# Quartering a second of the seven gate/up products in a FoX hybrid block on one Trainium2 core

## The chip, the cores and the metric

The kernel runs on one core of a Trainium2 chip. That core has a matrix engine (PE, with its weight loads shown as PEld), three engines for elementwise work (VectorE, called DVE in the profile; ScalarE, called ACT; GpSimd, called POOL), and a queue for transfers that SyncE (SP) issues. Matmuls write into banks of PSUM, an accumulator memory; everything else lies in SBUF, or in DRAM. Each engine works through its own queue in the order of the program, and waits there for the others.

The metric is the device time of one execution in microseconds. The kernel before takes 1034.87 us, the median of three runs (1034.17 to 1035.08).

## The reference

One layer on x of 1024 rows by 1024 channels, in float32:

```python
h = rmsnorm(x, norm1_g)
proj = einsum('bsd,de->bse', h, w_in)        # q, k, v, f_logit, u
attn = forgetting_attention(q, k, v, log_sigmoid(f_logit + b_forget))
pool = multiscale_pool(u, w_pool, pool_scale)
x = x + einsum('bse,ed->bsd', concat(attn, pool), w_out)
h2 = rmsnorm(x, norm2_g)
gate = einsum('bsd,df->bsf', h2, w_gate)     # w_gate, w_up: 1024 x 2816
up = einsum('bsd,df->bsf', h2, w_up)
x = x + einsum('bsf,fd->bsd', silu(gate) * up, w_down)
return rmsnorm(x, final_g)
```

The change concerns `gate`, `up` and `silu(gate) * up`, and the sums of the latter on which the product with `w_down` works.

## The kernel before

**Precision.** A float32 product is made of three matmuls in a reduced format: each operand is split into a high half (a copy in that format, on ACT, L120) and a low half (the operand less its high half, on DVE, L121). `mm3` multiplies high by high, low by high and high by low (L161 to L163).

**The gate/up product.** The 2816 channels are taken in 11 pairs `j` of 2 x 128 channels. For each pair, the weights are a 2 x 2 matrix of blocks `a11`, `a12`, `a21`, `a22` (by pair half and by half of the 1024 inputs; each 128 x 2 x 512, gate and up side by side), and the activations are a 2 x 2 matrix of blocks too (by input half and by half of the rows). One level of Strassen-Winograd makes the pair's output with seven products P1 to P7 instead of eight. P1, P2 and P4 take weight blocks as they are; P5, P6, P7 and P3 take sums `s1` to `s4` of them (L1070 to L1073, on POOL). A product has two parts, gate (n = 0) and up (n = 1), of twelve matmuls of 512 columns each. Its moving side is a block of activations, split once for all pairs (`b11`, `b21`, `t2`, `t3`, `t1`, `b22`, `t4`); its weights are a *page* of high and low halves, made per pair. Three pages rotate.

**Quartering.** From pair 1 on, P3 is again cut into seven fine products Q1 to Q7, by the same scheme, 42 matmuls of 256 columns in all. Their weights are two smaller pages, P3a (four quarters: Q1, Q2, Q7, Q4) and P3b (three: Q5, Q3, Q6), whose sums are made in place in `s4` (L1213). Each fine product is added by DVE from its PSUM bank into a snapshot in SBUF (L1249).

**Banks, snapshots, corners.** P1, P6, P5 accumulate in the bank pair `c1`; after each of them ACT copies the banks into a snapshot (`sn`: `sP1`, `sU2`, `sU4`; L1135). P2 has the banks `c2`, P7 and P4 the banks `c3`. The four corners of a pair's output (`h11`, `h12`, `h21`, `h22`) are the snapshots plus a bank: DVE adds gate and up (L1154, L1156), ACT applies silu to the gate (L1155), POOL multiplies (L1157). The down product needs, by the same scheme, the corners and their sums `f1` to `f4` (L1161, on POOL). All are sent to DRAM (`hsd`) by DMAs that ACT's queue issues (`spill`, L1254).

**The order.** The program lists for each pair `LATER = P1 P2 P6 P7 P5 P3a P4 P3b`, and walks through it. At each step it makes the page of the step after next (`next_page`), issues spills, emits the step's matmuls, and then the corners that have become complete (`after`). P4 and the fine products of P3 are laid among each other by hand. `tc.issue_after` pins an instruction behind another in its queue; otherwise each engine runs the instructions in the order in which the program emits them. Raw weights are loaded per half (`gu_raw`), by SP's queue.

**Around it.** Before the pairs come the input projection, attention, pooling and the output projection; after them come the down product and the last norm. The change touches there only which tiles the row buffers and the first down pages use.

## Time and profile before

| | before |
|---|---|
| median of three runs | 1034.87 us |
| the profiled execution's time | 1035.78 us |
| its span in the profile | 1034.0 us |
| PE busy | 1022.9 us, 99% |
| DVE busy | 711.6 us, 69% |
| ACT busy | 465.2 us, 45% |
| POOL busy | 405.4 us, 39% |
| granted TensorE clock, mean | 0.998 |
| time in DMA queue q1 (weights, corners, rows) | 33.0% of 16 engines |

The span is the time between the first and the last record; the execution's own time is 1.78 us longer. A line of a timeline gives the start and duration in us, the engine, the line in the kernel, the operation with what it writes and reads, and in brackets how long the engine was idle before and what ended that. A line of the windows gives, for PE, PEld, DVE, ACT and POOL, the busy time and (in brackets) how many instructions began, and at its end the granted clock, the share of DMA and GB/s. A line of the waits gives who waited for whom: us in total, how often, and the longest. A duration in a timeline is from an instruction's start to its end; the next one of the same engine can start a little before that.

### The profile page before, as it was taken

The numbers are of one execution on the slowest core, as the hardware profiler recorded it, in microseconds if no ns is written. First come the engines' busy times: TensorE is split into PE (matmuls) and PEld (weight loads), VectorE is DVE, ScalarE is ACT, GpSimd is POOL, SyncE is SP. The second block draws the span as 40 slices with busy tenths as digits, with TensorE's granted clock in tenths as the row PEclk, the third lists the DMA queues.
The fourth block names the chain that finished last, engine by engine and source line by source line (L and its number), as shares of the span: only waits on it lengthen the run. The fifth ranks groups of instructions, "written<-read, shape, count | busy, mean of one in ns | idle before, by whom it ended". The sixth has DMA issues, their size and how long they took to land.

```text
span 1034.0 us, 14701 instructions
## 1 busy us (share of the span) xinstructions
PE 1022.9 (99%) x5284; PEld 873.6 (84%) x5284; DVE 711.6 (69%) x1131; ACT 465.2 (45%) x747; POOL 405.4 (39%) x316
## 2 busy tenths in 40 slices
PE   8999999999999999999999999999999999999997
PEld 7988888998888888888888888888888888888885
DVE  7565566776886479786565455556547899788886
ACT  7434355665665257533343333433334343333346
POOL 4350121213346043356558548557558410000045
PEclk9999999999999999999999999999999999999999
DMA  7214424333743133333242243233326665352424
GB/s 251 53 47 144 105 80 106 82 103 86 234 166 104 49 132 112 93 112 102 102 142 101 65 142 106 79 122 112 92 102 254 214 254 181 119 188 94 153 92 163
DMA packets 108249, 130.25 MB, mean 126 GB/s; under 512 B 7368, under 2 KB 70352, under 8 KB 108176
## 3 DMA queue, kind: packets, MB, share of 16 engines
q1 hardware_dynamic: 96544, 108.18, 33.0%
q10 hardware_dynamic: 11072, 19.69, 5.0%
q0 software_dynamic: 560, 1.44, 0.4%
q8 instruction: 42, 0.69, 0.3%
q14 instruction: 31, 0.25, 0.1%
HBM read 86.29 MB, written 33.03 MB: 115 GB/s over the span
## 4 chain that ended last, share of the span: by engine, by line
PE 49%; DVE 2%; DMA 1%; issue 1%; POOL 1%; ACT 0%; SPq 0%; POOLq 0%; ACTq 0%; DVEq 0%
PE gu_P L163 9%; PE gu_P L162 9%; PE gu_P L161 9%; PE d L162 5%; PE d L163 5%; PE d L161 5%; DMA r_wd<-in_w_down_dram 1%; DVE d L121 1%; DVE x2f_s L1533 0%; DMA r<-in_w_up_dram 0%; POOL f L1161 0%; DMA hsdP<-f 0%; DVE gu_P_l L121 0%; POOL h L1157 0%; POOL hsdP L1254 0%
## 5 line engine op out<-in xcount | busy, mean ns | idle before, releaser
L162 PE MATMUL d<-d,d 128*128 128x512 f32 (+1 forms) x308 | 118.8, 389 | 0.5 <-DVE d L121 0.5
L163 PE MATMUL d<-d,d 128*128 128x512 f32 (+1 forms) x308 | 118.5, 388 | 0.0
L629 POOL TENSOR_SCALAR p<-p,rr 128x128 f32<-128x128 f32 (+3 forms) x64 | 48.5, 763 | 177.0 <-DVE rr L628 135.9
L161 PE MATMUL d<-d,d 128*128 128x512 f32 x308 | 107.8, 388 | 0.0
L120 ACT ACTIVATE d<-r_f 128x1536 fp32r<-128x1536 f32 (+1 forms) x28 | 38.7, 1383 | 109.6 <-PE d L162 106.0
L1157 POOL TENSOR_TENSOR h<-h,qh 128x512 f32<-128x512 f32 x33 | 64.5, 1955 | 34.8 <-ACT qh L1155 26.9
L1070 POOL TENSOR_TENSOR s<-r 128x1024 f32<-128x1024 f32 x10 | 24.0, 2397 | 133.0 <-DMA r<-in_w_up_dram 86.9
L121 DVE TENSOR_TENSOR gu_P_l<-r,gu_P_h 128x1024 fp32r<-128x1024 f32 x32 | 52.8, 1651 | 31.9 <-ACT gu_P_h L120 31.9
L120 ACT ACTIVATE gu_P_h<-r 128x1024 fp32r<-128x1024 f32 x32 | 33.8, 1060 | 85.9 <-issue 43.4
L162 PEld LDWEIGHTS d<-d,d 128*128 128x128 f32 x308 | 57.8, 188 | 13.3 <-DVE d L121 1.4
L1438 POOL TENSOR_SCALAR sse<-sse 128x1 f32<-128x1 f32 x7 | 3.5, 494 | 167.3 <-ACT junk L1434 167.3
L161 PEld LDWEIGHTS d<-d,d 128*128 128x128 f32 x308 | 57.8, 188 | 12.0
L163 PEld LDWEIGHTS d<-d,d 128*128 128x128 f32 x308 | 57.8, 188 | 11.8
L121 DVE TENSOR_TENSOR gu_P_l<-s,gu_P_h 128x1024 fp32r<-128x1024 f32 (+1 forms) x38 | 51.8, 1371 | 18.9 <-ACT gu_P_h L120 18.8
L626 ACT ACTIVATE p<-p,mn 128x128 f32<-128x128 f32 (+3 forms) x64 | 49.4, 772 | 32.3 <-DVE mn L620 29.4
L648 DVE TENSOR_TENSOR tl<-tp,th 128x512 fp32r<-128x512 f32 (+1 forms) x80 | 49.5, 633 | 9.7 <-ACT th L647 8.7
L121 DVE TENSOR_TENSOR d<-r_f,d 128x1536 fp32r<-128x1536 f32 (+1 forms) x28 | 47.7, 1705 | 6.2 <-ACT d L120 6.2
L163 PE MATMUL qk<-hTh,l_qk 128*128 128x512 f32 x128 | 50.7, 396 | 0.0
L161 PE MATMUL qk<-hTh,h_qk 128*128 128x512 f32 x128 | 50.6, 395 | 0.0
L162 PE MATMUL qk<-hTl,h_qk 128*128 128x512 f32 x128 | 50.4, 394 | 0.0
L1155 ACT ACTIVATE qh<-qh 128x512 f32<-128x512 f32 x33 | 20.9, 632 | 64.6 <-POOL f L1161 32.6
L1533 DVE TENSOR_TENSOR x2f_s<-d,x2f_s 128x512 f32<-128x512 f32 x64 | 42.5, 686 | 10.6 <-PE d L163 10.6
(802 smaller groups left out, 3235.8 us busy)
## 6 DMA issues: line engine op xcount, KB each, us to landing
r_f<-hsdP SPq DMA_DIRECT2D x77, 256.0 KB
r_wd<-in_w_down_dram SPq DMA_DIRECT2D x22, 512.0 KB
r<-in_w_gate_dram SPq DMA_DIRECT2D x21, 512.0 KB
r<-in_w_up_dram SPq DMA_DIRECT2D x21, 512.0 KB
hsdP<-f ACTq DMA_DIRECT2D x40, 256.0 KB
s<-hi SPq DMA_DIRECT2D x64, 128.0 KB
hsdP<-h ACTq DMA_DIRECT2D x32, 256.0 KB
x<-in_x_dram SPq DMA_DIRECT2D x8, 512.0 KB
```

The costliest lines, as they stand in the source:

```text
L120: mark["hi"] = nc.scalar.activation(out=hi, in_=src, func=AF.Copy)
L121: return eng.tensor_tensor(out=lo, in0=src, in1=f32(hi), op=ALU.subtract)
L161: nc.tensor.matmul(ps, lh, rh, start=start, stop=False, **kw)
L162: nc.tensor.matmul(ps, lh, rl, start=False, stop=False, **kw)
L163: mark["mm"] = nc.tensor.matmul(ps, ll, rh, start=False, stop=stop, **kw)
L626: nc.scalar.activation(out=pr[:, :n], in_=pr[:, :n], func=AF.Exp, scale=-1.0, bias=mn, accum_out=rs)
L629: nc.gpsimd.tensor_scalar(out=pr[:, :n], in0=pr[:, :n], scalar1=rr, scalar2=1.0, op0=ALU.mult, op1=ALU.mult)
L648: nc.vector.tensor_tensor(out=tl[:, :w], in0=tp[:, :w], in1=f32(th[:, :w]), op=ALU.subtract)
L1070: g(out=s1, in0=a21, in1=a22, op=ALU.add)
L1155: nc.scalar.activation(out=q, in_=q, func=AF.Silu)
L1157: nc.gpsimd.tensor_tensor(out=h, in0=h, in1=q, op=ALU.mult)
L1533: added = nc.vector.tensor_tensor(out=row, in0=ps, in1=row, op=ALU.add)
```

## The change

- **P4 is quartered like P3**, in pairs 2 to 10. Pair 1, whose P3 was quartered before, now has seven whole products. The fine pieces of P4 are laid among the matmuls of P7, those of P3 among P5's (`PIECES`). The order of a pair is now `P2 P1 P6 P4a P7 P4b P3a P5 P3b`.
- **The fine products' banks.** Q1, Q6 and Q5 share a bank (A), Q7 and Q4 one (B), Q2 and Q3 one (C). For P4, A and B come from the rotating pair `m`, and C is P2's first bank; for P3, A is P2's second bank and B and C come from `m`. Q5 is added into two targets instead of one. P4's fine products are added into the snapshot `sU2`; those of P3 into a new pair of tiles `acc`, four of them by a copy on ACT (L1270) and the others by DVE (L1273).
- **The corners are made in place**: the snapshot takes the bank's add (`add_bank`, L1310), the silu (L1318) and POOL's product (L1319), with no tile of its own.
- **The weight sums move from POOL to DVE** and are made in place in the raw blocks, in two pairs: `small_sums` (L1069, L1070) at the pair's start, `large_sums` (L1076, L1077) two steps later. `s` serves P6 and then P3; `a21` becomes P7's operand, `a11` P5's.
- **Raw weights are loaded block by block** as their homes become free.
- The quartered block of P4's moving side (`t4`) is made on DVE as `b22`'s is, in pair 1, and `b22`'s after it.

```diff
-    LATER = ("P1", "P2", "P6", "P7", "P5", "P3a", "P4", "P3b")
-    todo = [(j, k) for j in range(NG) for k in (LATER if j else FIRST)]
+    LATER = ("P2", "P1", "P6", "P4a", "P7", "P4b", "P3a", "P5", "P3b")
+    todo = [(j, k) for j in range(NG) for k in ((FIRST, PRODUCTS)[j] if j < 2 else LATER)]
...
+    PIECES = (
+        ("Q1", "Q2", "Q7", (0, (0, 1)), "Q4"), ((0, (2, 3)), "Q6", (1, (0, 1)), (1, (2, 3))), ("Q3", "Q5"),
+    )
...
-        elif i and (k in ("P3a", "P3b") or k == "P4" and j):
+        elif j > 1 and in_pair > 2:
+            small, whole = (("P4", "P7"), ("P3", "P5"))[in_pair > 5]
...
+            acc = snaps[j, "sU2" if small == "P4" else "acc"]
+            for piece in PIECES[in_pair % 3]:
```
```diff
-    def gu_sums(j):
+    def small_sums(j):
+
         a11, a12, a21, a22 = gu_parts(j)
-        s1, s2, s3, s4 = (xw_tile(f"s{i}", f"s{i}_{j}", (P, 2, 512)) for i in (1, 2, 3, 4))
-        g = nc.gpsimd.tensor_tensor
-        g(out=s1, in0=a21, in1=a22, op=ALU.add)
-        g(out=s2, in0=s1, in1=a11, op=ALU.subtract)
-        g(out=s3, in0=a11, in1=a21, op=ALU.subtract)
-        g(out=s4, in0=a12, in1=s2, op=ALU.subtract)
-        return dict(P1=a11, P2=a12, P6=s2, P7=s3, P5=s1, P3=s4, P4=a22)
+        both = xw_tile("s1", f"s_{j}")
+        operands[j].update(P6=both, P3=both)
+        nc.vector.tensor_tensor(out=a21, in0=a11, in1=a21, op=ALU.subtract)
+        nc.vector.tensor_tensor(out=both, in0=a22, in1=a21, op=ALU.subtract)
+
+    def large_sums(j):
+
+        a11, a12, _, _ = gu_parts(j)
+        both = operands[j]["P6"]
+        nc.vector.tensor_tensor(out=a11, in0=both, in1=a11, op=ALU.add)
+        nc.vector.tensor_tensor(out=both, in0=a12, in1=both, op=ALU.subtract)
```
```diff
-    FINE_BANK = dict(Q1="A", Q6="A", Q5="A", Q3="A", Q7="B", Q4="B", Q2="C")
-    FINE_TO = dict(Q1=(0, 0), Q2=(0, 0), Q7=(1, 1), Q4=(1, 0), Q6=(1, 0), Q5=(1, 1), Q3=(0, 1))
+    FINE_BANK = dict(Q1="A", Q6="A", Q5="A", Q7="B", Q4="B", Q2="C", Q3="C")
+    FINE_TO = dict(
+        Q1=((0, 0),), Q2=((0, 0),), Q7=((1, 1),), Q4=((1, 0),), Q6=((1, 0),), Q3=((0, 1),), Q5=((0, 1), (1, 1))
+    )
+    FINE_COPY = ("Q1", "Q7", "Q4", "Q3")
+    FINE_AT = dict(
+        P4=dict(A=("m", 2), B=("m", 2), C=(BANKS["c2", 0], 1)), P3=dict(A=(BANKS["c2", 1], 1), B=("m", 2), C=("m", 2))
+    )
...
+        for n, h in FINE_TO[q]:
+            out = acc[n][:, QTR[h]]
+            if k == "P3" and q in FINE_COPY:
+                nc.scalar.activation(out=out, in_=ps, func=AF.Copy)
+                continue
+            with tc.issue_after(mark["add"].ins) if "add" in mark else ExitStack():
+                mark["add"] = nc.vector.tensor_tensor(out=out, in0=ps, in1=out, op=ALU.add)
...
+    def gated(j, name, key, ts, src=None):
+
+        for n, t in enumerate(ts):
+            if src:
+                add_bank(t, src, n)
+            if n == 0:
+                nc.scalar.activation(out=t, in_=t, func=AF.Silu)
+        nc.gpsimd.tensor_tensor(out=ts[1], in0=ts[1], in1=ts[0], op=ALU.mult)
+        feats[name] = ts[1]
+        if key:
+            spills.append((hsd[key, j], ts[1]))
```

**Three places in the queues**, all in the middle pairs. A name holds its pair: `gu6_P5_l` is the low half of the page of P5 in pair 6, `fineA_6P4` the bank A of P4's fine products in pair 6; the last digits are a tile's number.

DVE, before, pair 6, from P4's low half through P3's fine adds to the next pair's P1:

```order
L121 TENSOR_TENSOR gu6_P4_l_6871<-r1_6_6575,gu6_P4_h_6870 128x1024
L1154 TENSOR_TENSOR qh22_6_6906<-gu6_P70_6844,sn6_sU40_6901 128x512
L1249 TENSOR_TENSOR sn6_sU40_6901<-fineA_6P3_6927,sn6_sU40_6901 128x256
L121 TENSOR_TENSOR gu6_P3b_l_6915<-s4_6_6622,gu6_P3b_h_6914 128x768
L1156 TENSOR_TENSOR h22_6_6905<-gu6_P71_6857,sn6_sU41_6903 128x512
L1249 TENSOR_TENSOR sn6_sU40_6901<-fineC_6P3_6935,sn6_sU40_6901 128x256
L1249 TENSOR_TENSOR sn6_sU41_6903<-fineB_6P3_6943,sn6_sU41_6903 128x256
L1249 TENSOR_TENSOR sn6_sU41_6903<-fineA_6P3_6927,sn6_sU41_6903 128x256
```

DVE, in the changed kernel, pair 6, from Q3 of P4 (bank C) to the first add of P3's fine products:

```order
L1273 TENSOR_TENSOR sn6_sU20_6993<-fineC_6P4_7015,sn6_sU20_6993 128x256
L121 TENSOR_TENSOR gu6_P5_l_7083<-a11_6_6748,gu6_P5_h_7082 128x1024
L1273 TENSOR_TENSOR sn6_sU20_6993<-fineA_6P4_7007,sn6_sU20_6993 128x256
L1310 TENSOR_TENSOR sn6_sU21_6994<-gu6_P71_7063,sn6_sU21_6994 128x512
L121 TENSOR_TENSOR gu6_P3b_l_7110<-s_6_6880,gu6_P3b_h_7109 128x768
L1273 TENSOR_TENSOR sn6_sU21_6994<-fineA_6P4_7007,sn6_sU21_6994 128x256
L1273 TENSOR_TENSOR acc6_0_7114<-fineC_6P3_7124,acc6_0_7114 128x256
```

Q5's two adds (bank A, rows 3 and 6) now stand with a page's low half ahead of the first, and an add from P7's bank and another low half between them. Q7 of P3 is the next to use bank A of P4.

DVE again, in the changed kernel, from the first low half of pair 7 to its second sum of weights:

```order
L121 TENSOR_TENSOR gu7_P2_l_7154<-a12_7_6958,gu7_P2_h_7153 128x1024
L1310 TENSOR_TENSOR sn6_sP70_7076<-gu6_P10_6922,sn6_sP70_7076 128x512
L1273 TENSOR_TENSOR acc6_1_7115<-fineA_6P3_7116,acc6_1_7115 128x256
L1310 TENSOR_TENSOR sn6_sP71_7077<-gu6_P11_6935,sn6_sP71_7077 128x512
L121 TENSOR_TENSOR gu7_P1_l_7187<-a11_7_7086,gu7_P1_h_7186 128x1024
L1069 TENSOR_TENSOR a21_7_6965<-a11_7_7086,a21_7_6965 128x1024
L1273 TENSOR_TENSOR acc6_0_7114<-fineA_6P3_7116,acc6_0_7114 128x256
L1273 TENSOR_TENSOR acc6_1_7115<-fineA_6P3_7116,acc6_1_7115 128x256
L1070 TENSOR_TENSOR s_7_7218<-a22_7_7004,a21_7_6965 128x1024
```

The same stretch before, from the next pair's P1 on:

```order
L121 TENSOR_TENSOR gu7_P1_l_6978<-r0_7_6841,gu7_P1_h_6977 128x1024
L1249 TENSOR_TENSOR sn6_sU41_6903<-fineA_6P3_6927,sn6_sU41_6903 128x256
L121 TENSOR_TENSOR gu7_P2_l_7001<-r0_7_6841,gu7_P2_h_7000 128x1024
L1213 TENSOR_TENSOR s4_7_6921<-s4_7_6921 128x256
L1249 TENSOR_TENSOR sn6_sU40_6901<-fineA_6P3_6927,sn6_sU40_6901 128x256
L1154 TENSOR_TENSOR qh21_6_7014<-gu6_P70_6844,sn6_sU20_6832 128x512
L1156 TENSOR_TENSOR h21_6_7013<-gu6_P71_6857,sn6_sU21_6834 128x512
L121 TENSOR_TENSOR gu7_P6_l_7028<-s2_7_6919,gu7_P6_h_7027 128x1024
```

The first sum of the pair's weights (L1069) has come in ahead of Q5's last two adds, whose bank is P2's second one.

ACT, before, from P1's second snapshot of pair 6 on to P3a's high half:

```order
L1135 ACTIVATE sn6_sP11_6765<-gu6_P11_6750 128x512
L1254 DMA hsdP2_5_4835<-h21_5_6714 128x512
L1254 DMA hsdP5_5_4868<-f1_5_6720 128x512
L1155 ACTIVATE qh11_6_6798<-qh11_6_6798 128x512
L1254 DMA hsdP6_5_4846<-f2_5_6722 128x512
L120 ACTIVATE gu6_P5_h_6803<-s1_6_6619 128x1024
L1254 DMA hsdP7_5_4857<-f3_5_6724 128x512
L1254 DMA hsdP3_5_4879<-f4_5_6726 128x512
L1135 ACTIVATE sn6_sU20_6832<-gu6_P10_6737 128x512
L1254 DMA hsdP1_6_4825<-h11_6_6797 128x512
L120 ACTIVATE gu6_P3a_h_6837<-s4_6_6622 128x1024
```

ACT, in the changed kernel, the same transfers of pairs 5 and 6:

```order
L1278 DMA hsdP5_5_4874<-f1_5_6872 128x512
L1306 ACTIVATE sn6_sP10_6948<-gu6_P10_6922 128x512
L1278 DMA hsdP6_5_4852<-f2_5_6874 128x512
L120 ACTIVATE gu6_P7_h_6961<-a21_6_6627 128x1024
L1278 DMA hsdP7_5_4863<-f3_5_6876 128x512
L1306 ACTIVATE sn6_sP11_6949<-gu6_P11_6935 128x512
L1318 ACTIVATE sn6_sP10_6948<-sn6_sP10_6948 128x512
L1278 DMA hsdP3_5_4885<-f4_5_6878 128x512
L1306 ACTIVATE sn6_sU20_6993<-gu6_P10_6922 128x512
L1278 DMA hsdP1_6_4831<-sn6_sP11_6949 128x512
L120 ACTIVATE gu6_P4b_h_7000<-a22_6_6666 128x768
L1306 ACTIVATE sn6_sU21_6994<-gu6_P11_6935 128x512
```

The transfer of f3 now stands ahead of P1's second snapshot instead of behind it, and the transfer of h11 (`hsdP1`) ahead of P4b's high half.

More of the change, by code (lines that the diff above doesn't have):

```diff
@@ L1205, in fine_steps, with own_temps, ring_temps @@
         ]
+    def own_temps():
+        pair = const.tile([P, 2, 2, 256], F32, tag="wmask", bufs=1, name="pair")
+        ends = [wk.tile([P, 2, 256], F32, tag=f"e{n}", bufs=1, name=f"end{n}") for n in range(2)]
+        return lambda c, h: (pair[:, h, :, :], ends[h])[c]
+    def ring_temps(c, h):
+        return wk_tile("h", 8, f"whole{c}{h}").rearrange("p (c t) -> p c t", c=2)
     def fine_page(j, k, part):
@@ L1288, in tile_kernel @@
     BANK3 = (("m", 2), ("m", 2), ("tp1", 1), ("po", 1))
-    PAGES = (("t3h", "t3l", "t1h", "t1l"), ("b22h", "b22l", "t4h", "t4l"))
+    PAGES = (("t3h", "t3l", "t4h", "t4l"), ("b22h", "b22l", "t1h", "t1l"))
     SUMS = dict(P5="b21h", P6="b21l", P7="t2h", P4="t2l")
@@ L1395, in tile_kernel @@
                     down_page(0)
[L1396 to L1399 removed]
+        if (j, k) == (1, "P1"):
+            fine_tiles("t4", dict(Q5=((xw, "s2"),), Q6=((xw, "s3"),), Q7=((xw, "s4"),)))
+            finer += fine_steps("t4", own_temps())
+        if (j, k) == (1, "P4"):
+            while finer:
+                finer.pop(0)()
+            fine_tiles("b22", dict(
+                Q5=((const, "wmask"),), Q6=((wk, "e0"), (wk, "e1")), Q7=((wk, "e2"), (xw, "junk2"))
+            ))
+            finer += fine_steps("b22", ring_temps)
+        for _ in range(min(3, len(finer) - (j == 1 and k != "P4"))):
+            with tc.issue_after(mark["page"].ins):
+                finer.pop(0)()
         pages.pop((j, k))
```

190 lines of the change are left out of this document (111 added, 79 removed).

## The prediction

> **What bounds the kernel now.** I read the page's sums first, then the windows by stage, then the timelines of one pair's stretch.
>
> ```profile
> span 1034.0 us, 14701 instructions
> PE 1022.9 (99%) x5284; PEld 873.6 (84%) x5284; DVE 711.6 (69%) x1131; ACT 465.2 (45%) x747; POOL 405.4 (39%) x316
> ...
> 649.73:687.51 37.78, 37.78 (x187) 32.05 (x187) 20.83 (x26) 13.91 (x19) 22.99 (x11) 1.00 0.32 105
> ...
> 800.00:1034.00 234.00, 226.16 (x1023) 187.44 (x1021) 200.44 (x209) 94.96 (x105) 40.60 (x45) 0.99 0.46 161
> ```
>
> PE is busy 1022.9 of 1034.0 us. One pair of the gate and up products lasts 37.78 us, in which PE never waits; DVE is busy 20.83, POOL 22.99, ACT 13.91, at a granted clock of 1.00. So only two things count here: the matmul time of a pair, and any new wait of PE.
>
> ```profile
> 653.42 0.39 PE L161 MATMUL gu_P<-t1h,gu_P_h 128*128 128x512 f32 x1
> ...
> 654.10 0.28 PE L161 MATMUL fineA_6P<-b22h,gu_P3a_h 128*128 128x256 f32 x1
> ...
> 654.69 0.28 PE L163 MATMUL fineA_6P<-b22h,gu_P3a_l 128*128 128x256 f32 x1
> ...
> 656.13 0.28 PE L163 MATMUL fineB_6P<-fine3h_b,gu_P3a_l 128*128 128x256 f32 x1
> 656.25 0.40 PE L161 MATMUL gu_P<-t4h,gu_P_h 128*128 128x512 f32 x1
> ```
>
> From 653.42 to 654.10 three whole matmuls start, 0.2275 us each; from 654.10 to 656.25 eighteen fine ones, 0.1195 each. A whole product is 24 × 0.2275 = 5.46 us, a quartered one 42 × 0.1195 = 5.02. Six and one make 37.78, the window.
>
> **What the quartering gains.** 5.46 - 5.02 = 0.44 us for each product. Pairs 2 to 10 quarter one more, pair 1 one less: 8 × 0.44 = 3.5 us, 0.34% of the time. A pair without waits is 5 × 5.46 + 2 × 5.02 = 37.34 us. That is all there is to win; one wait of 0.44 us in a pair takes it back.
>
> **What DVE gets.**
>
> ```profile
> 655.01 0.42 DVE L1249 TENSOR_TENSOR sn_sU<-fineA_6P,sn_sU 128x256 f32<-128x256 f32 x1 [2.04 <-PE fineA_6P L163]
> 655.36 0.95 DVE L121 TENSOR_TENSOR gu_P3b_l<-s,gu_P3b_h 128x768 fp32r<-128x768 f32 x1
> 656.22 0.69 DVE L1156 TENSOR_TENSOR h<-gu_P,sn_sU 128x512 f32<-128x512 f32 x1
> 656.82 0.42 DVE L1249 TENSOR_TENSOR sn_sU<-fineC_6P,sn_sU 128x256 f32<-128x256 f32 x1
> ...
> 670.92 1.22 DVE L121 TENSOR_TENSOR gu_P_l<-s,gu_P_h 128x1024 fp32r<-128x1024 f32 x1
> 672.05 1.79 DVE L1273 TENSOR_TENSOR sn_sU<-sn_sU,sn_sU 128x512 f32<-128x512 f32 x1
> ...
> 684.99 1.22 DVE L1213 TENSOR_TENSOR s<-s 128x256 f32<-128x256 f32 x3
> ```
>
> From start to start, in a row without gaps: low half of 1024 1.13, of 768 0.86; add from a bank of 512 0.60, of 256 0.34 (0.33 to 0.35); 256 out of SBUF 0.40 (1.22 for three, to the last one's end), taken as 0.34 from start to start. A sum of 1024 on DVE has no row; it has the low half's shape and two SBUF inputs, so I take 1.13 (bounds: 0.86, the low half of 768, and 2.08 us, what a low half of 1024 takes beside POOL, below). Per pair: 7 × 1.13 + 2 × 0.86 + 4 sums × 1.13 + 20 × 0.34 + 8 × 0.60 = 25.8 us of 37.3. DVE fits on average; the order of its queue decides. POOL loses four sums of 2.4 us a pair, which nothing waits for late today, so that is worth nothing by itself.
>
> **Wait 1: P3's Q7, 1.79 us a pair.** Q7 of P3 writes the bank that held Q1, Q6 and Q5 of P4, free after Q5's second add. Put Q3's end at 0. Row 654.69 ends at 654.97, 0.16 us behind the start of the next piece (654.81), and DVE starts at 655.01: so DVE starts at 0.20. In the queue then stand Q3's add 0.34, P5 low 1.13, Q5's first add 0.34, an add from P7's bank 0.60, P3b low 0.86, Q5's second add 0.42 to its end: 3.89. PE has Q5, Q1 and Q2 of 0.72 each, and is due at 2.15. With 0.05 of release it goes on at 3.94: **1.79 lost**. Nothing here hangs on a guess but the order, and DVE's rows run in it. In the kernel before, the fine products that use those banks next come a whole pair later, so there these adds have time.
>
> **The lock between DVE and POOL.**
>
> ```profile
> 661.03 1.30 POOL L1157 TENSOR_TENSOR h<-h,qh 128x512 f32<-128x512 f32 x1
> 662.28 3.39 POOL L1071 TENSOR_TENSOR s<-s,r 128x1024 f32<-128x1024 f32 x1
> 665.75 3.26 POOL L1073 TENSOR_TENSOR s<-r,s 128x1024 f32<-128x1024 f32 x1
> ...
> 677.47 1.29 POOL L1161 TENSOR_TENSOR f<-h,sn_sU 128x512 f32<-128x512 f32 x1
> ...
> 679.96 2.28 POOL L1157 TENSOR_TENSOR h<-h,qh 128x512 f32<-128x512 f32 x1
> ```
> ```profile
> 661.66 1.76 DVE L121 TENSOR_TENSOR gu_P_l<-r,gu_P_h 128x1024 fp32r<-128x1024 f32 x1 [0.60 <-ACT gu_P_h L120]
> ...
> 679.00 2.08 DVE L121 TENSOR_TENSOR gu_P_l<-s,gu_P_h 128x1024 fp32r<-128x1024 f32 x1 [2.15 <-ACT gu_P_h L120]
> ```
> ```profile
> 580.73 2.41 POOL L1070 TENSOR_TENSOR s<-r 128x1024 f32<-128x1024 f32 x1 [11.11 <-DMA r<-in_w_up_dram]
> ...
> 581.26 0.42 DVE L1249 TENSOR_TENSOR sn_sU<-fineC_4P,sn_sU 128x256 f32<-128x256 f32 x1
> ```
>
> A DVE low half that begins during a POOL operation ends some 1.1 us after that one (662.33 to 663.42), and POOL's next, of 3.39 instead of 2.4, ends late in its turn: they take turns by whole instructions. The add with a bank (581.26) beside POOL takes its plain 0.42. So each POOL operation of 1.25 us among DVE's two-SBUF-input operations can cost them up to 1.25 us. The Trainium skill ("SBUF — State Buffer", section "Who interferes with whom") says the same, an exclusive lock of the shared port pair for a whole instruction; by a shared bandwidth, its opposite, the forecast would be rival A's.
>
> **Wait 2: P2's second half, 1.0 us a pair.** Its bank is free after Q5's adds of the P3 before, which stand behind P1 low and the first sum. After wait 1, PE ends P5's last matmul at 11.71 and comes to P2's second half at 15.72 (3.94 + 5 fine products of 0.717 + 36 × 0.2275). DVE adds P5's bank at 11.75 to 12.43; POOL's gate product follows at 12.51, P1 low is ready at 12.6. If POOL comes first: 13.80 + 1.13 + 1.13 + 0.34 + 0.42 = 16.8, a loss of 1.0; if DVE does, 15.7 and none. I take POOL, as the earlier by 0.1 us, and keep both.
>
> **Wait 3, from the lock, 1.15, and wait 4 at P4's Q4, 2.4 us.**
>
> ```profile
> 645.19 0.33 ACTq L1254 DMA_DIRECT2D hsdP<-h  x1
> 645.57 1.06 ACT L120 ACTIVATE gu_P3a_h<-s 128x1024 fp32r<-128x1024 f32 x1 [1.62 <-POOL h L1157]
> ...
> 654.13 0.84 ACT L120 ACTIVATE gu_P3b_h<-s 128x768 fp32r<-128x768 f32 x1 [0.49 <-PE gu_P L162]
> ...
> ACT gu_P3a_h L120 <- POOL h L1157: 14.6, 9, 1.6
> ```
>
> Spills are issued from ACT's queue and wait for POOL; the next high half waits behind them (1.62 us here, nine times 14.6 in all, today hidden by pages made early). From 16.7 on, DVE has in order: a sum 1.13, two bank adds 1.20, 0.34, P6 low and P4a low 2.26, a sum 1.13, 0.34, a sum 1.13, then 0.34 × 3 and a bank add 0.60, P7 low 1.13, P1's second bank add 0.60: 10.9 us, to 27.6. Into it fall POOL's gate product and f1 to f4, five of about 1.1: 33.2. Two things follow. A spill of f3 on ACT stands ahead of the snapshot of P1's second bank, which P6's second half writes on: about 1.15 us. And POOL's product of h11 ends at 34.5, its spill holds ACT to 35.0, P4b high takes 0.75, P4b low 0.86, and Q2's and Q7's adds behind it 0.34 each: 37.4. PE needs Q7's bank, to write Q4, at 35.0: 2.4 lost. Bounds for both together: nothing, if POOL's operations fall into DVE's gaps; 5 × 1.25 more than now if all of them stretch it further.
>
> **The sum.** 37.34 + 1.79 + 1.0 + 1.15 + 2.4 = 43.7, against 37.78: 5.9 more, and for four restarts, whose first matmul takes 0.50 instead of 0.39 (below), some 0.1 in all: 6.0.
>
> ```profile
> 855.05 0.50 PE L162 MATMUL d<-d,d 128*128 128x512 f32 x1 [0.45 <-DVE d L121]
> ```
>
> 9 × 6.0 = 54. Pair 1 loses its quartering, 0.44. The quartering of the two blocks runs on DVE in pairs 1 and 2, some 25 operations of 512 at 0.6 to 1.8 us: 0 to 5 us seen by PE, 3.5 taken, as it lies in the queue ahead of page halves. At the last pair two column sums stand in DVE's queue: 0 to 2, 1 taken. Together 59. The profiled execution took 1035.78 us, 1.78 more than its span and 0.91 more than the median of 1034.87: 1035.78 + 59 - 0.91 = **1094 us**.
>
> **The rivals.** *A: only the waits that DVE's own order makes; the lock is absorbed.* For it: POOL has 10 us of work a pair instead of 23, and may slip between DVE's waits. Against it: the rows show strict turns, and POOL's five lie where DVE has no gap. 9 × (1.35 to 2.35) + 0.44 gives 1047 to 1056; with part of waits 3 and 4, up to 1075. *B, the other side: faster.* The place is P3's Q7: if the chain of six on DVE ended before 2.15 instead of 3.89, as it would with the two low halves (1.99) behind Q5's second add, wait 1 would be gone, and with waits 2 to 4 hidden 3.5 us remain: 1031. Against it: the order stands in the program, and a bank that is read late is not written early. The point of decision is 0.4 us of waits a pair: above it the result is slower. *C: longer.* More than the forecast's turns, or a lower clock: PE idles 14% of a pair. The last window of the first fence had 7.8 us of PE idle at a clock of 0.99, so short waits cost none there. If every pair lost 2 to 4 us more: 1112 to 1130. The Trainium skill ("TensorE: Matmul & The Clock Gate", "What's actually happening") halves the clock after an idle window of about 3.4 us; the longest wait that I forecast is 2.4 us, so by it none would fall into that, unless waits run together. That the quartering isn't done is no rival: the program's order has the fine matmuls.
>
> **How the numbers follow.** Forecast 65% (1075 to 1112, 1094 likeliest), A 18% (1047 to 1075), C 10%, B 5%, within 0.2% (about what a measurement can tell from no change) 2%. 1047 to 1112 leaves out 17%. Slower: 93%.
>
> **What would show it.** A window of one pair of 43 to 44 us with 37.3 of PE busy. In the waits: PE on a DVE add at P3's Q7 for 9 × 1.8 = 16 us; PE at P2 on DVE for 9; PE at P4's Q4 on DVE for 20 to 24; ACT behind POOL at spills. Matmul pitches unchanged. It would be wrong if Q7 starts within 0.5 us of Q2's end, if DVE's sums take other than 1.0 to 2.1 us, or if POOL's rows beside them show no stretch.

## The result, and the profile after

The changed kernel takes **1100.66 us** (median of six runs, 1099.47 to 1103.74), against 1034.97 us (six runs, 1034.17 to 1035.91) for the kernel before: a ratio of 1.064, with an interval of 1.0623 to 1.0658. It is 65.7 us slower. The forecast was 1094 us, with a range of 1047 to 1112.

The page's sums, and then the waits of PE as who waited for whom (us in total, times, longest):

```profile
span 1099.3 us, 15266 instructions
PE 1035.2 (94%) x5428; PEld 879.5 (80%) x5428; DVE 817.3 (74%) x1270; ACT 486.3 (44%) x795; POOL 318.6 (29%) x284
```
```profile
PE gu_P L161 <- ACT sn_sP L1306: 7.7, 9, 2.4
PE gu_P L161 <- DVE acc L1273: 7.2, 8, 0.9
PE fineB_10P L161 <- DVE sn_sU L1273: 5.7, 2, 3.8
...
PE fineB_6P L161 <- DVE sn_sU L1273: 4.0, 2, 2.4
```

Four kinds of wait are new. Each pair has two at bank B (`fineB`), one at P2's second half (for `acc`), and one at P6 (for P1's snapshot on ACT). PE's busy time rose too, by 12.3 us, though it has less matmul work: matmuls at half clock, and the matmuls on both sides of a wait, count for more (0.27 us a wait, below). DVE is busy 105.7 us longer and is at 74%, so it isn't the bound on average.

Now one pair, from P3's Q7 to the next one's. The PE timeline's waits between 645 and 690, where the bracket at a row's end is how long PE was idle before it, and the windows of this pair and the one after it:

```profile
645.35 0.39 PE L161 MATMUL fineB_5P<-fine_b22Q7h,gu_P3a_h 128*128 128x256 f32 x1 [1.62 <-DVE sn_sU L1273]
...
658.37 0.50 PE L161 MATMUL gu_P<-b21h,gu_P_h 128*128 128x512 f32 x1 [0.89 <-DVE acc L1273]
...
670.22 0.50 PE L161 MATMUL gu_P<-t2h,gu_P_h 128*128 128x512 f32 x1 [0.65 <-ACT sn_sP L1306]
...
679.14 0.39 PE L161 MATMUL fineB_6P<-t4h,gu_P4a_h 128*128 128x256 f32 x1 [2.35 <-DVE sn_sU L1273]
679.36 0.28 PE L162 MATMUL fineB_6P<-t4l,gu_P4a_h 128*128 128x256 f32 x1
```
```profile
645.35:689.46 44.11, 38.59 (x205) 32.33 (x205) 32.72 (x42) 16.04 (x23) 13.90 (x8) 1.00 0.28 90
689.46:734.98 45.52, 39.99 (x205) 33.51 (x205) 32.83 (x42) 16.04 (x23) 13.90 (x8) 0.96 0.27 88
```

A pair lasts 44.11 us instead of 37.78, at a granted clock of 1.00, and PE idles in exactly four places: P3's Q7, P2's second half, P6, P4's Q4. The second pair is 1.4 us longer at a clock of 0.96, with nearly the same work on the other engines; that is taken up at the end.

The chains behind three of the waits are plain in the same stretch. First POOL, then DVE, then ACT, of the changed kernel:

```profile
654.14 1.30 POOL L1319 TENSOR_TENSOR sn_sP<-sn_sP,sn_sP 128x512 f32<-128x512 f32 x1 [7.32 <-DVE sn_sP L1310]
...
667.68 1.48 POOL L1164 TENSOR_TENSOR f<-sn_sP,acc 128x512 f32<-128x512 f32 x1
...
674.81 1.29 POOL L1319 TENSOR_TENSOR sn_sP<-sn_sP,sn_sP 128x512 f32<-128x512 f32 x1 [3.42 <-issue]
```
```profile
654.23 2.28 DVE L121 TENSOR_TENSOR gu_P_l<-a,gu_P_h 128x1024 fp32r<-128x1024 f32 x1 [0.22 <-ACT gu_P_h L120]
656.44 1.21 DVE L1069 TENSOR_TENSOR a<-a,a 128x1024 f32<-128x1024 f32 x1
657.58 0.74 DVE L1273 TENSOR_TENSOR acc<-fineA_5P,acc 128x256 f32<-128x256 f32 x2
...
664.27 2.31 DVE L1076 TENSOR_TENSOR a<-s,a 128x1024 f32<-128x1024 f32 x1
666.50 1.51 DVE L1228 TENSOR_TENSOR a<-a 128x256 f32<-128x256 f32 x1
...
677.46 0.96 DVE L121 TENSOR_TENSOR gu_P4b_l<-a,gu_P4b_h 128x768 fp32r<-128x768 f32 x1 [2.45 <-ACT gu_P4b_h L120]
```
```profile
668.18 1.06 ACT L120 ACTIVATE gu_P_h<-a 128x1024 fp32r<-128x1024 f32 x1 [1.69 <-POOL f L1164]
...
669.57 0.60 ACT L1306 ACTIVATE sn_sP<-gu_P 128x512 f32<-128x512 f32 x1 [0.32 <-PE gu_P L163]
...
676.58 0.84 ACT L120 ACTIVATE gu_P4b_h<-a 128x768 fp32r<-128x768 f32 x1 [3.16 <-POOL sn_sP L1319]
```

- **P2:** POOL's product begins 0.09 us ahead of P1's low half (654.14 against 654.23); the low half then takes 2.28 us. Behind it stand the first sum (L1069, 1.21) and Q5's two adds (657.58, done at 658.32): PE starts at 658.37.
- **P6:** on ACT the transfer of f2 waits for POOL. P7's high half stands behind it (668.18 to 669.24), then the transfer of f3, which POOL has ready at 669.16 (667.68 and 1.48) and which is issued by 669.52, then P1's second snapshot at 669.57; PE starts at 670.22. The bracket of that snapshot names PE, but P1's last matmul began before 666.67. ACT's own queue held it, and f3 in a second way too: the snapshot is written into the tile in which the pair before made h11 in place, and f3 reads that tile until 669.16.
- **Q4:** POOL's product of h11 (674.81) ends at 676.10. ACT has waited 3.16 us for it, with P4b's high half behind the transfer (676.58), and P4b's low half follows at 677.46, ahead of the adds that free bank B.

A sum that has DVE to itself takes 1.21 (L1069); beside POOL it takes 2.31 (L1076).

### The profile page after: what moved, and what is told of

Same layout as the page of the kernel before. It is cut to its first block, busy times and chain, and to the rows that moved or that the text cites. A ratio compares the mean times of both kernels' runs of the same rounds, so it can differ in the third digit from the quotient of the medians.

```text
span 1099.3 us, 15266 instructions
## 1 busy us (share of the span) xinstructions
PE 1035.2 (94%) x5428; PEld 879.5 (80%) x5428; DVE 817.3 (74%) x1270; ACT 486.3 (44%) x795; POOL 318.6 (29%) x284
## 3 DMA queue, kind: packets, MB, share of 16 engines
q0 software_dynamic: 480, 1.18, 0.3%
## 5 line engine op out<-in xcount | busy, mean ns | idle before, releaser
L121 DVE TENSOR_TENSOR gu_P_l<-a,gu_P_h 128x1024 fp32r<-128x1024 f32 x43 | 59.8, 1392 | 35.1 <-ACT gu_P_h L120 35.0
L120 ACT ACTIVATE gu_P_h<-a 128x1024 fp32r<-128x1024 f32 x43 | 45.5, 1059 | 68.4 <-PE gu_P L162 34.8
L1319 POOL TENSOR_TENSOR sn_sP<-sn_sP,sn_sP 128x512 f32<-128x512 f32 x18 | 26.2, 1457 | 105.7 <-DVE sn_sP L1310 58.1
L647 ACT ACTIVATE th<-tp 128x512 fp32r<-128x512 f32 (+1 forms) x80 | 42.5, 550 | 15.8 <-PE tp L643 12.7
L1629 DVE TENSOR_TENSOR x2f_s<-d,x2f_s 128x512 f32<-128x512 f32 x51 | 34.1, 685 | 15.4 <-PE d L163 15.4
L1319 POOL TENSOR_TENSOR sn_sU<-sn_sU,sn_sU 128x512 f32<-128x512 f32 x9 | 12.1, 1347 | 112.2 <-DVE sn_sU L1273 94.5
L620 DVE CUSTOM_DVE_ANT_0 p<-z,wmask 128x128 f32<-128x128 f32 (+3 forms) x64 | 33.7, 534 | 13.6 <-PE z L618 9.7
```

What stands on the lines that cost most here:

```text
L120: mark["hi"] = nc.scalar.activation(out=hi, in_=src, func=AF.Copy)
L121: return eng.tensor_tensor(out=lo, in0=src, in1=f32(hi), op=ALU.subtract)
L620: nc.vector.tensor_tensor_reduce(out=pr[:, n0:n1], in0=z, in1=wmask[:, S - n + n0 : S - n + n1], scale=1.0, scalar=mn, op0=ALU.add, op1=AL ...
L647: nc.scalar.activation(out=th[:, :w], in_=tp[:, :w], func=AF.Copy)
L1319: nc.gpsimd.tensor_tensor(out=ts[1], in0=ts[1], in1=ts[0], op=ALU.mult)
L1629: added = nc.vector.tensor_tensor(out=row, in0=ps, in1=row, op=ALU.add)
```

## The experiments

The theory was that of the prediction: the waits come from the order of DVE's and ACT's queues (Q7, P2, and the transfers on ACT) and from DVE and POOL taking turns. The rival: DVE simply has too much to do in a pair, and mending one place only moves the wait. First, single parts were undone, one per kernel. Where no number of runs stands, a time is that of one run; the kernel before took 1036.71 us beside the first four kernels and 1035.2 beside the next four.

**P3's Q7 later by one piece.** Two matmul groups of P5's first half now stand ahead of Q7 instead of behind it.

```diff
+    PIECES3 = ("Q1", "Q2", (0, (0, 1)), "Q7", "Q4")
-            for piece in PIECES[in_pair % 3]:
+            for piece in PIECES3 if k == "P3a" else PIECES[in_pair % 3]:
```

> Only P3's Q7 moves, behind the first half of P5's gate matmuls (6 x 0.2275 = 1.37 us later). Theory (Q7 waits for a bank that DVE's add of Q5 frees 3.89 us after Q3's end, whatever PE does): the wait at P3's Q7 shrinks from 1.62 us shown to about 0.3 in each of nine pairs, the other three waits keep their length (0.89, 0.66, 2.36), a pair takes 42.7 us instead of 44.1: about 1088 us, 1084 to 1091. Rival (DVE has too much work, and a wait taken away comes back at the next place): P2's or Q4's wait grows by as much, 1096 to 1102.

It took 1100.86 us, no gain, and not the 1084 to 1091 expected. Two of its waits on PE's timeline, and the windows of two pairs:

```profile
602.68 0.38 PE L161 MATMUL fineB_4P<-fine_b22Q7h,gu_P3a_h 128*128 128x256 f32 x1 [0.24 <-DVE sn_sU L1273]
...
604.13 0.38 PE L161 MATMUL fineB_4P<-b22h,gu_P3a_h 128*128 128x256 f32 x1 [0.47 <-ACT acc L1270]
```
```profile
602.68:646.15 43.47, 38.85 (x204) 32.25 (x204) 32.72 (x42) 16.05 (x23) 13.89 (x8) 1.00 0.28 91
646.15:691.15 45.00, 40.38 (x204) 33.47 (x204) 32.81 (x42) 16.03 (x23) 13.87 (x8) 0.96 0.27 88
```

The mechanism is as argued: Q7's wait fell from 1.62 to 0.24. But Q4 of P3 now waits 0.47 for ACT's copy of Q7, and a pair at full clock won only 0.64 us (43.47 against 44.11). Eight such gains, 5 us, are what this profile then lost again: it has six stretches of some 3.4 us at half clock where the changed kernel has three, and each costs about 1.4 to 1.5 us (45.00 against 43.47). So the gain at one wait went into the clock. The time is the rival's, its reason only in part: the new wait at P3's Q4 took back half of what Q7 won, but in pairs 3 to 9 neither P2's wait (0.89) nor that at P4's Q4 (2.33 to 2.37) grew.

**The transfers issued from SP's queue instead of ACT's.**

```diff
-    def spill(q=nc.scalar):
+    def spill(q=nc.sync):
```

> The transfers of the corners and their sums are issued by SP's queue instead of ACT's. Theory (ACT stands behind the transfers that wait for POOL, so that P1's second snapshot and P4b's high half are late): the waits at P6's second half (0.66) and at P4's Q4 (2.36) go to under 0.1 and under 0.8; 9 x 2.3 to 3.2 us less and no half-clock stretches: 1068 to 1080 us. Rival (the lock with POOL alone makes DVE late, ACT is late only because DVE is): Q4's wait stays over 1.8 and the time over 1090.

1082.07 us: 18.6 us faster than the changed kernel, and 2 above the expected range. The wait at P4's Q4 is gone, and a pair lasts 42.03 us (639.69 to 681.72). Yet P6 waits longer, 1.22 instead of 0.65, where under 0.1 was expected. PE's row and what ACT does before it:

```profile
665.10 0.50 PE L161 MATMUL gu_P<-t2h,gu_P_h 128*128 128x512 f32 x1 [1.22 <-ACT sn_sP L1306]
```
```profile
662.99 0.63 ACT L1318 ACTIVATE sn_sP<-sn_sP 128x512 f32<-128x512 f32 x1 [3.85 <-DVE sn_sP L1310]
663.53 1.04 ACT L120 ACTIVATE gu_P_h<-a 128x1024 fp32r<-128x1024 f32 x1
664.47 0.58 ACT L1306 ACTIVATE sn_sP<-gu_P 128x512 f32<-128x512 f32 x1
```

With the transfers off its queue, ACT waits 3.85 us with a silu that needs DVE's bank add; a high half and P1's second snapshot stand behind it. The head of ACT's queue changed, and DVE, late because of the turns with POOL, is now what it waits for.

**POOL's four sums of the features left out.**

```diff
-            feature_sum(j, "f1", "P5", "h12", "h22", ALU.add)
-            feature_sum(j, "f2", "P6", "f1", "h11", ALU.subtract)
-            feature_sum(j, "f3", "P7", "h11", "h12", ALU.subtract)
-            feature_sum(j, "f4", "P3", "h21", "f2", ALU.subtract)
+            for key in ("P5", "P6", "P7", "P3"):
+                spills.append((hsd[key, j], feats["h12"]))
```

> POOL's four sums f1 to f4 are left out for pairs 2 to 10 (the corner h12 is sent four times in their place), and the transfers stay on ACT. Theory (DVE's rows of two SBUF inputs are stretched by POOL's rows): DVE's low half of P4a, its weight sums and the quarter sums beside them go from 2.0, 2.3 and 1.5 us to about 1.2 and 0.4, 4 to 5 us a pair; the waits at P6's second half and Q4 go below 0.3; Q7's and P2's waits stay: 1068 to 1078 us. Rival (the stretch comes from something else, DMA traffic or DVE's own instructions): the rows keep 2.0 to 2.3 us and Q4's wait stays over 1.5; above 1085 us.

1070.42 us. In pairs 3 to 9 the waits at P6 and Q4 are gone, those at Q7 (1.62) and P2 (0.89) are as they were, and a pair lasts 40.52. DVE's rows show why:

```profile
656.78 1.21 DVE L1076 TENSOR_TENSOR a<-s,a 128x1024 f32<-128x1024 f32 x1
657.92 0.41 DVE L1228 TENSOR_TENSOR a<-a 128x256 f32<-128x256 f32 x1
```

The same two operations took 2.31 and 1.51 us beside POOL, 1.1 us more each, as did the two that follow them there (2.32 and 1.50). So waits 3 and 4 hang on these sums, and waits 1 and 2 don't (of POOL's work wait 2 needs only the gate product, which is still there). They do it by the turns and because ACT's transfers wait for them (and P1's snapshot for f3), which this kernel doesn't separate; of the 3.6 us that a pair lost here (44.11 to 40.52), the kernel with the transfers on SP won 2.1 with the turns in place.

**The pair's first two sums behind Q5's adds.**

```diff
-        with tc.issue_after(mark["page"].ins):
+        with tc.issue_after(mark["add" if i == 0 and j > 2 else "page"].ins):
```

> The first sum of a pair's weights is put behind Q5's two adds of the P3 before, instead of ahead of them. Theory: P2's wait (0.89) falls below 0.1. What PE gains there is lost again or not at P6 and Q4, whose waits hang on DVE's whole queue: those two together between 1 us less and 1 us more a pair, 1085 to 1101 us. Rival (P2's bank is late for another reason): the wait stays over 0.6.

1088.59 us. P2's wait is gone, as the order of the queue has it, and P6's and Q4's fell to 0.34 and 1.01; P7's low half is late by 0.49 instead. Single edits thus do what the prediction's chains say, and each leaves or makes another wait. The rival's second half holds.

**Q7 of P3 two pieces later**, alone, to see whether Q7's gain can be kept:

```diff
+    PIECES3 = (
+        ("Q1", "Q2", (0, (0, 1)), (0, (2, 3)), "Q7", (1, (0, 1)), "Q4"), ("Q6", (1, (2, 3))), ("Q3", "Q5"),
+    )
+            PIECES = PIECES3 if in_pair > 5 else PIECES4
```

> Among P5's matmuls alone the fine pieces move: both halves of P5's gate part ahead of P3's Q7, a half of the up part between Q7 and Q4. Theory (Q7 waits for the bank and Q4 for the copy of Q7, at fixed times): both waits go to nothing, P2's (0.89), P6's (0.66) and Q4's of P4 (2.36) stay; a pair without a half-clock stretch takes 42.3 us instead of 44.1, 1085 us with three such stretches of 1.4, each further one 1.4 more: 1081 to 1092. Rival (DVE has too much work in all, so that any wait taken away comes back): a pair stays over 43.5.

1087.3 us, in the expected range, but by luck: the waits aren't those expected. Those at Q7 and Q4 of P3 are gone, and so is the one at P4's Q4 in pairs 3 to 9, which was to stay; but P2's second half now waits 2.28 us instead of 0.89, and P6 1.18 to 1.47 instead of 0.65:

```profile
611.28 0.50 PE L161 MATMUL gu_P<-b21h,gu_P_h 128*128 128x512 f32 x1 [2.28 <-DVE acc L1273]
```

PE reaches P2's second half some 1.9 us sooner, and Q5's adds come only 0.5 sooner (both against the start of P4's Q5): in DVE's queue they now stand behind both of the pair's first sums. Eight stretches at half clock, at a mean of 0.986, took a further part.

**Four mends at once**: both products' pieces later, the transfers on SP, the sums behind the adds. Its edits are those shown, and for P4:

```diff
+    PIECES4 = (
+        ("Q1", "Q2", "Q7", (0, (0, 1)), (0, (2, 3)), "Q4"), ("Q6", (1, (0, 1)), (1, (2, 3))), ("Q3", "Q5"),
+    )
```

> All together: fine pieces of P3 and P4 moved behind whole ones, first sum behind Q5's adds, spills on SP's queue. Theory (four waits with four causes, the lock of 5 us a pair still there): waits at Q7, P2 and P6 under 0.1; at P4's Q4 0.5 to 1.5, because DVE's chain from P5's end to Q7's add takes 23.8 us with the lock and PE is there in 22.7; 38.0 to 39.0 us a pair, 1038 to 1052 us. Rival (DVE's 25.8 us and the lock fill the pair): over 40 us a pair, above 1062.

1060.81 us, above what was expected. A pair lasts 39.64 (681.90 to 721.54); P2's wait stayed, and Q4 waits 0.48. PE, and DVE in the same place:

```profile
680.11 0.28 PE L161 MATMUL fineA_6P<-fine_b22Q,gu_P3b_h 128*128 128x256 f32 x1
...
681.90 0.50 PE L161 MATMUL gu_P<-b21h,gu_P_h 128*128 128x512 f32 x1 [0.92 <-DVE acc L1273]
```
```profile
681.09 0.76 DVE L1273 TENSOR_TENSOR acc<-fineA_6P,acc 128x256 f32<-128x256 f32 x2 [2.04 <-PE fineA_6P L163]
```

DVE was idle and added at once; it is PE that runs Q5 (680.11) late, right before P2's second half, which needs Q5's bank. That is an order of PE's queue, and no mend on DVE can reach it.

**No work of POOL in the pairs.** As the kernel above, with gate products and feature sums of pairs 2 to 10 on DVE:

```diff
-        nc.gpsimd.tensor_tensor(out=t, in0=feats[a], in1=feats[b], op=op)
+        (nc.vector if j > 1 else nc.gpsimd).tensor_tensor(out=t, in0=feats[a], in1=feats[b], op=op)
-        nc.gpsimd.tensor_tensor(out=ts[1], in0=ts[1], in1=ts[0], op=ALU.mult)
+        nc.vector.tensor_tensor(out=ts[1], in0=ts[1], in1=ts[0], op=ALU.mult)
```

> As the four mends, and the gate products and f1 to f4 of pairs 2 to 10 on DVE, POOL idle. Theory (each POOL operation of 512 costs DVE 1.1 us by the lock, and 0.60 as an operation of its own): DVE's rows of two SBUF inputs take 1.13 to 1.22 again, DVE is busy 30 to 31 us a pair, Q4's wait goes below 0.3, 37.3 to 37.8 us a pair, 1031 to 1043 us with what pairs 2 and 10 keep. Rival (work counts, not the lock: 4.8 us more on DVE): slower than the four mends, above 1045.

1052.91 us, 7.9 less, though DVE has eight more operations in every pair. A pair lasts 38.59 (675.84 to 714.43). It is above the 1031 to 1043 expected: P2's wait of 0.92 is still in every pair, and the last pair waits 3.7 at Q4. The rival had it slower than the four mends, which it isn't.

```profile
683.05 1.22 DVE L121 TENSOR_TENSOR gu_P4a_l<-a,gu_P4a_h 128x1024 fp32r<-128x1024 f32 x1
684.18 1.22 DVE L1076 TENSOR_TENSOR a<-s,a 128x1024 f32<-128x1024 f32 x1
...
685.92 0.68 DVE L1164 TENSOR_TENSOR f<-sn_sU,f 128x512 f32<-128x512 f32 x1
686.52 0.42 DVE L1228 TENSOR_TENSOR a<-a 128x256 f32<-128x256 f32 x1
```

The same low half and sum took 2.31 each in the kernel with POOL. A feature sum costs DVE 0.60 from start to start (685.92 to 686.52) when it does it itself, and 1.1 when POOL does it. This speaks against the first half of the rival: with more work on DVE a pair is shorter. That DVE can do all of it in a pair without a wait is shown by the kernel with Q5's order mended, below. So it is the turns and the order, and not the amount of work.

**The opposite: the two large sums back on POOL**, with the four mends, and ACT's snapshots pinned in the order of the program:

```diff
-        nc.vector.tensor_tensor(out=a11, in0=both, in1=a11, op=ALU.add)
-        nc.vector.tensor_tensor(out=both, in0=a12, in1=both, op=ALU.subtract)
+        nc.gpsimd.tensor_tensor(out=a11, in0=both, in1=a11, op=ALU.add)
+        nc.gpsimd.tensor_tensor(out=both, in0=a12, in1=both, op=ALU.subtract)
```

> As the four mends, and the two large weight sums of a pair back on POOL (2.4 us each), the snapshots pinned in their order on ACT. Theory (the lock is strict turns, and longer POOL operations block DVE for longer, but out of Q4's chain come 2.3 us of sums): Q4's wait below 0.5 and 37.4 to 38.3 us a pair, 1033 to 1047 us; DVE's rows beside the large sums go to 2.5 to 3.5 us. Rival (longer turns eat what leaves the queue): Q4's wait over 1.0, above 1047.

This expectation fell: 1110.58 us. P6 waits 4.95 us (46.5 in all), with a stretch at half clock behind it in every pair. POOL's longer operations hold DVE, and DVE holds ACT's silu, but ACT is through with that and with P7's high half at 675.69. Then it is idle for 2.86 us, until f3 has read the tile that P1's second snapshot is written into; and f3 is late because the two large sums stand ahead of it on POOL. PE, then ACT, then POOL:

```profile
679.20 0.80 PE L161 MATMUL gu_P<-t2h,gu_P_h 128*128 128x512 f32 x1 [4.95 <-ACT sn_sP L1307]
```
```profile
674.65 1.04 ACT L120 ACTIVATE gu_P_h<-a 128x1024 fp32r<-128x1024 f32 x1
678.55 0.60 ACT L1307 ACTIVATE sn_sP<-gu_P 128x512 f32<-128x512 f32 x1 [2.86 <-POOL f L1164]
```
```profile
677.08 1.44 POOL L1164 TENSOR_TENSOR f<-sn_sP,acc 128x512 f32<-128x512 f32 x1
```

**The order of Q5 mended too.** To the kernel without POOL in the pairs: P2's matmuls behind Q5's, the steps of `b22`'s quartering behind pair 2's snapshots, the last pair's column sums one step later and behind its adds, its feature sums on POOL.

```diff
-                product(j, k, n)
+                with tc.issue_after(mark["mm"].ins) if j > 2 and k == "P2" else ExitStack():
+                    product(j, k, n)
-            if k == "P6":
+            if k == "P5":
...
+                    with tc.issue_after(mark["add"].ins):
+                        down_sum(0, key)
...
+        for _ in range(min(0 if (j, k) == (2, "P2") else 3, len(finer) - (j == 1 and k != "P4"))):
+            with tc.issue_after(mark["page" if j < 2 else "snap"].ins):
```

> As the run without POOL, and: P3's Q5 pinned ahead of the next P2 (P2's wait of 0.92 was for Q5's adds, when Q5 came right before P2's second half), the block b22 quartered behind pair 2's snapshots, two column sums of the last pair later, the last pair's feature sums on POOL. Theory (only the order of the queues and the lock cost time; the quartering itself saves 0.44 us a product): no wait of PE over 0.3 in pairs 3 to 9, 37.34 us a pair, 1030 to 1038 us. Rival (DVE at 30.5 us a pair can't serve PE in 37.3): a new wait of 0.4 or more in each pair, 38 us and more, above 1040.

1045.44 us (four runs, 1042.8 to 1045.79), a ratio of 1.0096 (1.0079 to 1.0112) to the kernel before, and above the 1030 to 1038 expected. PE has no wait left in pairs 3 to 10, and of this kernel's edits only the pin of P2 behind Q5 touches the middle pairs. So that order was P2's last cause. The rival's wait in each pair isn't there, though the time is in its range. What remains stands at the ends: in pair 2, 0.8 us at P6 and 4.2 at P4's Q4, where the block's quartering fills DVE's queue, and the start of the down product.

Three versions then moved the quartering of `b22` in part into pair 1 (all three), and the last pair's column sums to different places: behind P5, as above; behind P7; or one each behind P7 and P3a. The first, with the sums behind P5:

```diff
+        if (j, k) == (1, "P5"):
+            fine_tiles("b22", dict(Q5=((const, "wmask"),)))
+            b22_steps = fine_steps("b22", ring_temps)
+            now = [b22_steps[n] for n in (0, 1, 2, 3, 4, 5)]
+        if (j, k) == (1, "P3"):
+            fine_tiles("b22", dict(Q7=((wk, "e2"), (xw, "junk2"))))
+            now = [b22_steps[n] for n in (6, 7, 9, 10)]
```

> The same, with the last pair's column sums where the run with the order mended has them, late in pair 10. Theory: pair 2 as in the run before this one; the down product's first waits (1.3 + 0.5 + 0.7) stay: 1036 to 1041 us. Rival as before.

1039.21 us (four runs), a ratio of 1.0037 (1.0024 to 1.0051). Its window of a pair, and its two longest kinds of wait:

```profile
621.03:658.53 37.50, 37.50 (x205) 32.63 (x204) 31.03 (x49) 15.86 (x23) 0.00 (x0) 1.00 0.32 106
```
```profile
PE gu_P L161 <- ACT sn_sP L1306: 2.4, 1, 2.4
PE d L162 <- DVE d L121: 2.2, 2, 1.3
```

Here a pair is shorter than before, 37.50 against 37.78 with PE busy throughout: this is what the change can win, 0.28 us a product and not the 0.44 of the bare pitches. Nine such pairs win 2.5 us. One wait of 2.4 in pair 2, and pair 1's whole P3, take that back: from the first gate/up matmul (395.81 here, 396.66 before) to the first of the down product (814.88, 815.76) it is 419.07 us, and was 419.10. The waits of 2.2 and 1.2 us in the down product, for pages made late, 0.5 before, are what is left of the loss.

With the sums behind P7:

```diff
-            if k == "P6":
+            if k == "P7":
```

> As the run with the order mended, and the quartering of b22 moved from pair 2 into pair 1, where DVE has gaps; the last pair's two column sums behind P3a's low half. Theory (what is left over the kernel before are pair 2's waits of 4.2 and 0.8, the half clock after them, 1.5, and the end's 2.9): pair 2 without a wait over 0.3, some 0 to 2 us of waits in pair 10, 1032 to 1039 us. Rival (the b22 steps cost the same wherever they stand): pair 1 or 2 keep 3 us and more, above 1041.

1038.52 us (seven runs), a ratio of 1.003 (1.0018 to 1.0042): the down product waits no more than before (0.5), but the last pair's P5 waits 2.35 for its low half. DVE's rows ahead of that low half (it starts at 809.34) hold two operations of the column sums, of which the first is shown, and a step that takes 0.41 alone and here took 2.49 beside POOL:

```profile
803.99 1.21 DVE L1371 TENSOR_TENSOR sumP<-r_wd 128x1024 f32<-128x1024 f32 x1
...
806.93 2.49 DVE L1228 TENSOR_TENSOR s<-s 128x256 f32<-128x256 f32 x1
```

With one sum behind each of P7 and P3a, and the last two steps of `b22` behind pair 2's snapshots:

```diff
+            if k == "P7":
+                with tc.issue_after(mark["add"].ins):
+                    down_sum(0, "P5")
+            if k == "P3a":
+                with tc.issue_after(mark["add"].ins):
+                    down_sum(0, "P6")
```

> As the two runs before, with the last two steps of b22's quartering behind pair 2's snapshots (its wait of 2.4 and the half clock after it, 1.5) and the last pair's two column sums split, one ahead of P5's low half and one behind it (its wait of 2.35 becomes about 1.2, and the down product's first pages keep their order). Theory (what stands between this schedule and the kernel before are only such single waits): 1032 to 1036 us, 0.998 to 1.001 of the kernel before; pairs 2 to 9 without a wait over 0.3. Rival (new waits at the ends, as in each version so far): 1037 us and more.

1043.57 us (five runs), 1.0075 (1.0062 to 1.0089), worse than either and above the 1032 to 1036 expected: new waits at the ends, as its rival had it. Pair 2 waits twice (0.67 and 2.76) and the last pair 2.55. No version beat the kernel before.

## Why the prediction held, and where its sizes were off

By its own terms, for a pair. A record of a matmul ends 0.16 us behind the next one's start in an unbroken row, so 0.16 is added to each idle time of the profile.

| term | forecast, us | measured, us |
|---|---|---|
| matmuls of a pair | 37.34 | 37.50 |
| wait 1, Q7 of P3 | 1.79 | 1.62 + 0.16 = 1.78 |
| wait 2, P2's second half | 1.0 | 0.89 + 0.16 = 1.05 |
| wait 3, P6 | 1.15 | 0.65 + 0.16 = 0.81 |
| wait 4, Q4 of P4 | 2.4 | 2.35 + 0.16 = 2.51 |
| restarts | 0.1 | 4 x 0.11 = 0.44 |
| sum | 43.8 | 44.09 (a window of 44.11) |

- **Waits 1, 2 and 4** hold in place and size, and their chains run as written: with the start of P4's Q5 at 0 (641.41, as 2.15 us of three fine products behind P3's end had it), Q7 was to go on at 3.94 and did (645.35); P2's second half was to go on at 16.8 and went on at 16.96, POOL's product of h11 was to end at 34.5 and ended at 34.69, Q4 was to go on at 37.4 and went on at 37.73. The choice in wait 2, POOL ahead of DVE by 0.1 us, came out by 0.09; with so little between them, that it came out at all is in part luck, and by the forecast the other order would have left no wait there. The kernel with Q7 later showed the chain of wait 1, that with the sums behind the adds that of wait 2, those with SP's queue and without the feature sums that of wait 4.
- **Wait 3** has its place, and was 0.3 too long; the forecast gave its 1.15 without a sum. The transfer of f3 does stand ahead of the snapshot, but most of the delay came with that of f2 and P7's high half behind it. And the forecast lacked a path: the tile that f3 reads until 669.16. In the kernel with the four mends, whose transfers aren't on ACT, ACT is idle for 1.13 us and takes that snapshot at 652.78, 0.03 behind f3's end; so moving the transfers alone doesn't free it. A sum on DVE, taken as 1.13 us between 0.86 and 2.08, has 1.14 from start to start alone (656.44 to 657.58) and 2.23 beside POOL (664.27 to 666.50). That is over the 2.1 which the forecast named as a sign of being wrong; it holds for the two large sums, and is the 1.13 with one turn of POOL's, 1.1, which the forecast counted apart.
- **The gain of 0.44** is the term that was too large: 0.28 in an undisturbed pair. Restarts were too small, 0.11 each: the first pitch after a wait is 0.22 instead of 0.12 (679.14 to 679.36). Together with the waits this makes 0.33 us a pair more. That is less than the single errors, because wait 3's goes the other way: in this the sum was lucky. A pair is thus 0.1 above the 43 to 44 that the forecast named, and PE is busy 38.59 of it instead of 37.3: 37.50 and 4 x 0.27.
- **Of rival C, the lower clock did occur.** The forecast had no half clock at waits of 2.4 us; there are three stretches of it.
- **The rest of the misfit.** The profile's span grew by 65.3, against 59. From pair 2's Q7 to the last pair's, eight pairs took 55.5 more where 8 x 6.0 = 48 were forecast: 8 x 0.33 = 2.6 by the terms above, 1.4 by half clock in one pair, and 3.3 in the last, where Q4 waited 3.8 instead of 2.4 and half clock followed. The three small terms (0.44, 3.5 and 1) and the ninth pair, 10.9 together in the forecast, came to 9.8; what each of them took stays open.
- **Rival A** fell because POOL's few operations did lie where DVE has no gap: only the kernel without the feature sums, at 1070 us, falls into A's wider range. **Rival B** needed waits below 0.4 us a pair: four of them stand in the profile, and even the versions without a wait in most pairs stayed slower than before.

The Trainium skill ("SBUF — State Buffer", "Who interferes with whom") has DVE and POOL exclude each other for whole instructions where both inputs of DVE's lie in SBUF; the runs agree, 2.31 us beside POOL and 1.21 without it for the same sum.

## What to carry to other kernels

A rearrangement that saves 0.3 us of matmul time in a pair needs each bank, snapshot and page to be ready on time in every pair and also at the ends; so count, for each bank that is written sooner than before, what stands in the reader's queue ahead of the read that frees it, and for each tile that is made in place, who still reads it when it is to be written again. An operation given to POOL isn't free where DVE works on two SBUF inputs: here it cost DVE 1.1 us a piece, and 0.60 when DVE did it itself. When a wait is mended, look at what the profile shows next at the same engine's head: of the single mends here, all but the one that left out work made or lengthened another wait, or lost the gain to the clock.
